# Small parts of plain weight tiles by a subtraction on VectorE, or by an accumulating transfer onto the negated large part

## Chip, cores and metric

The kernel runs on one core of a Trainium2 chip. The metric is the device time of one execution in microseconds (us), as the median of several runs.

## What is computed

A two-layer encoder trunk for 512 tokens of width 1024, all in float32. Layer 0 uses stick-breaking attention, layer 1 forgetting attention (a softmax with a running sum of log forget gates), both with 16 heads of width 64. Each layer ends with a gated feed-forward part of width 2816 that has a causal convolution of width 3. Every part is normalized before and after (RMS), and added to the residual. Cut to what matters here:

```python
a = rmsnorm(h, sb_pre_g[0])
q, k, v = split(a @ sb_w_qkv[0], 3)
h = h + rmsnorm(attention(q, k, v) @ sb_w_o[0], sb_post_g[0])
f = conv_ffn(rmsnorm(h, ffn_pre_g[0]), w_up[0], conv_w[0], conv_b[0], w_down[0])
h = h + rmsnorm(f, ffn_post_g[0])
# layer 1: q from fox_w_q (with its own norm gain), k, v and gates from w_kvf, then fox_w_o and conv_ffn
# conv_ffn(x): gate, up = split(conv(x @ w_up) + b);  (gelu(gate) * up) @ w_down
```

## The kernel before

TensorE multiplies in a fast float32 format that keeps fewer bits. To keep float32's accuracy each factor is split into two parts, a rounded large part and the small rest, and each product is made in three passes: large by large, large by small, small by large. Activations are held as AH and AL, weights as `whi` and `wlo`.

The weights come as a stream of 196 tiles of 512 KB (list `stream`, built at lines 163 to 186). A column tile holds 128 output columns for all 1024 input rows (128 partitions x 8 x 128); for the values two tiles of 4 x 256 stand in place of it. A row tile holds 128 input rows and all 1024 output columns, one run of 4 KB per partition. Row tiles serve the output projections (`sb_w_o`, `fox_w_o`) and the down-projections (`w_down`). Of the 196 tiles 172 are plain: 24 of `sb_w_qkv`, 8 of `sb_w_o`, 88 of `w_up`, 44 of `w_down`, 8 of `fox_w_o`. The 24 others (`fox_w_q`, `w_kvf`) are scaled by a norm's gain as they are split.

`make` (line 127) makes one tile: SP starts the load into `raw` (two buffers), ScalarE rounds it into `whi` (line 142), and the small part is `raw - whi`, in two halves (line 146), on VectorE, or on GpSimd for rows 1, 5 and 7 of an output projection. `whi` and `wlo` have eight buffers each (`NW`). `take` (line 157) hands a tile out and asks for the one eight further on, so tiles are made up to eight ahead, as buffers come free. A `raw` buffer is free once both parts are made.

The stages of a layer: values, queries and keys are projected (`project_v`, `project`) between the heads' steps (`head`), which alternate between TensorE, ScalarE and VectorE. Then `out_proj` runs by token blocks 0 to 3; its eight row tiles are all held to the last block. After each block, the post-norm and the next pre-norm follow, whose inverse root is computed by two small GpSimd instructions (lines 217 and 218) before VectorE and TensorE go on. The up-projection begins with three chunks over the first 256 tokens, which need blocks 0 and 1 alone. The down-projection takes one row tile per 24 matmuls.

The order of instructions on each engine is set by a scheduler that goes by a simulated timeline; on the chip each engine takes its own in that order.

Of the kernel before, what the change touches and what calls it, by code (L numbers as in the profile page):

```python
# [14 lines left out]
P = 128  # L15
# [12 lines left out]
NW = 8  # L28
EARLY = 3
POOL_ROWS = (1, 5, 7)  # L30
FILL = (4, 5)
SCALE = HD**-0.5
# Column offset of each query block's row of scores, and its width.
# [4 lines left out]
def f32(ap):  # L38
    return ap.bitcast(F32)
# [3 lines left out]
def tile_trunk(  # L43
# [29 lines left out]
    # All of PSUM, by banks. Attention: scores 0-2, weighted values 3, projections 4-5, transposes 6-7.  # L73
    # Elsewhere: pairs of banks, one for each token block or chunk of features in flight.
# [15 lines left out]
    # mask_a keeps keys before the query, mask_b those up to it.  # L90
# [10 lines left out]
    # Residual stream by token blocks; normalized activations, feature-major, in two parts.  # L101
# [9 lines left out]
    # Row p stands for head p % 16 and is of kind p % 64 // 16: kinds 0, 2 or 3, 1; less 2, 0 or 1, less 3.  # L111
# [3 lines left out]
    # ---- weight stream: each tile arrives whole and is split into two exact parts. Pool takes few of them:  # L115
    # it and DVE's operations on two operands in SBUF exclude each other. ----
# [3 lines left out]
    def col_tile(w, c0, n=P, k0=0, nk=KT, g=None):  # L120
        src = w.rearrange("(k p) c -> p k c", p=P)[:, k0 : k0 + nk, c0 : c0 + n]
        return (src, nk, n, None if g is None else g + k0, nc.vector)

    def row_tile(w, k, eng=nc.vector):
        return (w[k * P : (k + 1) * P, :].rearrange("(a p) c -> p a c", p=P), 1, D, None, eng)

    def make(i):
        src, nk, n, g, eng = stream[i]
        raw = wp.tile([P, nk, n], F32, name=f"raw{i}", tag="raw", bufs=2)
        hi = wp.tile([P, nk, n], F32R, name=f"whi{i}", tag="whi", bufs=NW)  # L130
        lo = wp.tile([P, nk, n], F32R, name=f"wlo{i}", tag="wlo", bufs=NW)
        nc.sync.dma_start(raw, src)
        if g is not None:
            for k in range(nk):
                s = gcol[:, g + k : g + k + 1]
                nc.scalar.activation(hi[:, k], raw[:, k], AF.Copy, scale=s)  # L136
                nc.vector.scalar_tensor_tensor(
                    out=lo[:, k], in0=raw[:, k], scalar=s, in1=f32(hi[:, k]), op0=ALU.mult, op1=ALU.subtract
                )
            made[i] = (hi, lo)  # L140
            return
        nc.scalar.copy(hi, raw)  # L142
        h = (nk * n) // 2
        fr, fh, fl = (t.rearrange("p k c -> p (k c)") for t in (raw, f32(hi), lo))
        for s in (slice(0, h), slice(h, 2 * h)):
            eng.tensor_tensor(out=fl[:, s], in0=fr[:, s], in1=fh[:, s], op=ALU.subtract)  # L146
        made[i] = (hi, lo)
# [22 lines left out]
    stream += [row_tile(sb_w_o[0], k, nc.gpsimd if k in POOL_ROWS else nc.vector) for k in range(KT)]  # L170
# [14 lines left out]
    stream += [row_tile(fox_w_o[0], k, nc.gpsimd if k in POOL_ROWS else nc.vector) for k in range(KT)]  # L185
    stream += ffn_stream(1)

# [27 lines left out]
    def rstd_of(ss):  # L215
        """(sum / D + eps) ** -0.5 of ss's first column, into its column 3."""
        nc.gpsimd.tensor_scalar(ss[:, 2:3], ss[:, 0:1], 1.0 / D, EPS, op0=ALU.mult, op1=ALU.add)  # L217
        nc.gpsimd.tensor_tensor(out=ss[:, 3:4], in0=ss[:, 2:3], in1=mhalf, op=ALU.pow)
        return ss[:, 3:4]

    def pre_block(b, g, t4, junk):
        """Normalizes block b of the residual and puts it into AH and AL."""
# [14 lines left out]
    def post_block(b, y, g, t4, junk):  # L237
        """Adds the normalized y to block b of the residual."""
# [8 lines left out]
    def finish(b, y, g, t4, junk):  # L247
        """post_block for the last block, by halves, with its way out."""
# [22 lines left out]
    class Attn:  # L271
# [19 lines left out]
        def gates(self):  # L291
            """Running sums of the log forget gates, and what adds fcum[t] - fcum[s] to a head's scores:
            rows (fcum in two parts, 1, 1) by query times rows (1, 1, -fcum in two parts) by key, the rows
            of all heads, 16 to a kind, in both halves of the partitions."""
# [43 lines left out]
        def gate_keys(self, p):  # L338
            """The rows by key of pair p's heads."""
            KL = self.qk[p][3]  # L340
            for o, h in ((slice(64, 128), 0), (slice(0, 64), 1)):
                s = dsel[o, 2 * p + h : 2 * p + h + 1]
                nc.gpsimd.tensor_scalar(KL[o, h, :], f32(self.MV[o]), s, 1.0, op0=ALU.mult, op1=ALU.mult)
# [56 lines left out]
        def head(self, p, hh):  # L400
# [38 lines left out]
            else:  # L439
                # exp(z), guarded where sigmoid(z) is 1 and its complement under float32's rounding.  # L440
# [79 lines left out]
    def out_proj(done, heads_end):  # L520
        """Block by block, around the last head's transposes and products."""
# [187 lines left out]
```

## Time and profile before

| what | us |
|---|---|
| median of 3 runs | 1287.02 (1283.43 to 1288.18) |
| span of the profiled execution, first to last instruction | 1282.6 |
| TensorE busy in it | 1241.5 |
| VectorE busy | 811.0 |
| ScalarE busy | 644.4 |
| GpSimd busy | 101.8 |

Of the profiled execution the span alone is recorded; it lies 4.4 us under the median. In the rows below PE is TensorE's matmuls, PEld its weight loads, DVE VectorE, ACT ScalarE, POOL GpSimd, SP the engine that starts the transfers; L146 is line 146 of the kernel. `a<-b` names the tile written and those read. Behind an arrow in square brackets stands what ended an engine's idle time, with its length ahead of it.

### The profile page before, as it was taken

Reading aid. Unit: us, or ns where it says so; the run is one execution under the profiler, and the core shown is the slowest. Engines: PE = TensorE matmul, PEld = TensorE weight load, DVE = VectorE, ACT = ScalarE, POOL = GpSimd, SP = SyncE. Lnnn points to the kernel's source line nnn. Section 1 sums busy time; section 2 is a strip of 40 time slices with the busy share of each in tenths; the row PEclk is TensorE's granted clock in tenths of the full one; section 3 lists DMA queues with packets and bytes.
Section 4 is the critical chain, followed back from the end, with each engine's and each line's share of the span. In section 5 each row is a group of like instructions: output and inputs, shape, how many; then the busy total and the mean of one; then the engine's idle time right before and its main releaser. Section 6 shows DMA issues by size and latency. Waiting matters only on the chain.

```text
span 1282.6 us, 16820 instructions
## 1 busy us (share of the span) xinstructions
PE 1241.5 (97%) x6485; PEld 1054.6 (82%) x6485; DVE 811.0 (63%) x1304; ACT 644.4 (50%) x1085; POOL 101.8 (8%) x163
## 2 busy tenths in 40 slices
PE   6999998999999999999989999999999999999998
PEld 6888886789888888888888988978988888888886
DVE  6898899576655555433478887874685555554323
ACT  5767677454433333322488786674453333333221
POOL 1000003020000000000011212342100000000001
PEclk9999999999999999999999999999999999999999
DMA  6421212124333333333223122110543233323311
GB/s 214 138 66 50 67 50 66 33 86 144 101 97 99 92 90 99 88 109 90 75 68 99 51 82 67 50 51 33 148 132 98 84 97 99 94 87 98 99 33 66
DMA packets 145928, 111.97 MB, mean 87 GB/s; under 512 B 4680, under 2 KB 136120, under 8 KB 145848
## 3 DMA queue, kind: packets, MB, share of 16 engines
q1 hardware_dynamic: 145848, 110.90, 28.8%
q8 instruction: 51, 0.84, 0.3%
q14 instruction: 29, 0.24, 0.1%
HBM read 108.79 MB, written 2.10 MB: 86 GB/s over the span
## 4 chain that ended last, share of the span: by engine, by line
PE 77%; DVE 10%; ACT 5%; DMA 4%; issue 2%; POOL 0%; SPq 0%; DVEq 0%; POOLq 0%; ACTq 0%
PE PS L211 45%; PE PS L511 21%; PE PS L389 4%; PE PS L468 2%; PE PS L409 2%; DVE wlo L146 2%; DMA raw<-sb_w_qkv_dram 2%; DVE ec L446 2%; PE PS L456 2%; DMA raw<-w_up_dram 2%; DVE ec L448 1%; DVE PL L463 1%; ACT whi L142 1%; ACT whi L136 1%; ACT ec L445 1%
## 5 line engine op out<-in xcount | busy, mean ns | idle before, releaser
L211 PE MATMUL PS<-AH,whi 128*128 128x512 f32 (+1 forms) x1088 | 402.0, 370 | 5.5 <-DVE QS L360 3.8
L211 PE MATMUL PS<-AL,whi 128*128 128x512 f32 (+1 forms) x1088 | 401.2, 369 | 0.0
L211 PE MATMUL PS<-AH,wlo 128*128 128x512 f32 (+1 forms) x1088 | 401.0, 369 | 0.0
L146 DVE TENSOR_TENSOR wlo<-raw,whi 128x512 fp32r<-128x512 f32 x332 | 217.4, 697 | 224.5 <-ACT whi L142 223.7
L142 ACT CAST whi<-raw 128x1024 fp32r<-128x1024 f32 x172 | 180.4, 1049 | 237.9 <-PE PS L211 186.4
L211 PEld LDWEIGHTS PS<-AH,whi 128*128 128x128 f32 x1088 | 204.8, 188 | 43.5 <-DVE QS L360 4.9
L211 PEld LDWEIGHTS PS<-AH,wlo 128*128 128x128 f32 x1088 | 204.5, 188 | 36.7
L211 PEld LDWEIGHTS PS<-AL,whi 128*128 128x128 f32 x1088 | 204.8, 188 | 36.2
L587 DVE SCALAR_TENSOR_TENSOR hc<-PS,cw,hc 128x511 f32<-128x511 f32 (+1 forms) x176 | 130.7, 746 | 2.7
L511 PE MATMUL PS<-whi,al 128*128 128x512 f32 x352 | 109.5, 389 | 0.0
L511 PE MATMUL PS<-whi,ah 128*128 128x512 f32 x352 | 109.3, 389 | 0.0
L511 PE MATMUL PS<-wlo,ah 128*128 128x512 f32 x352 | 109.3, 389 | 0.0
L610 DVE TENSOR_TENSOR al<-act,ah 128x512 fp32r<-128x512 f32 x44 | 30.4, 690 | 117.4 <-ACT ah L609 117.4
L609 ACT CAST ah<-act 128x512 fp32r<-128x512 f32 x44 | 27.4, 622 | 144.7 <-PE PS L511 138.5
L217 POOL TENSOR_SCALAR ss<-ss 128x1 f32<-128x1 f32 x31 | 11.7, 376 | 830.9 <-ACT junk L240 764.8
L389 PE MATMUL PS<-whi,AH 128*128 128x256 f32 x256 | 74.1, 289 | 3.5 <-DVE AL L235 1.4
L511 PEld LDWEIGHTS PS<-whi,ah 128*128 128x128 f32 x352 | 66.1, 188 | 13.7
L511 PEld LDWEIGHTS PS<-whi,al 128*128 128x128 f32 x352 | 66.1, 188 | 13.7
L511 PEld LDWEIGHTS PS<-wlo,ah 128*128 128x128 f32 x352 | 66.1, 188 | 13.7
L389 PE MATMUL PS<-wlo,AH 128*128 128x256 f32 x256 | 74.0, 289 | 0.0
L389 PE MATMUL PS<-whi,AL 128*128 128x256 f32 x256 | 73.5, 287 | 0.0
L592 ACT ACTIVATE hc<-hc 128x512 f32<-128x512 f32 x44 | 27.8, 631 | 86.3 <-DVE hc L587 86.3
(130 smaller groups left out, 1758.9 us busy)
## 6 DMA issues: line engine op xcount, KB each, us to landing
raw<-w_up_dram SPq DMA_DIRECT2D x88, 512.0 KB
raw<-w_down_dram SPq DMA_DIRECT2D x44, 512.0 KB
raw<-sb_w_qkv_dram SPq DMA_DIRECT2D x24, 512.0 KB
raw<-w_kvf_dram SPq DMA_DIRECT2D x16, 512.0 KB
raw<-sb_w_o_dram SPq DMA_DIRECT2D x8, 512.0 KB
raw<-fox_w_q_dram SPq DMA_DIRECT2D x8, 512.0 KB
raw<-fox_w_o_dram SPq DMA_DIRECT2D x8, 512.0 KB
H<-x_dram SPq DMA_DIRECT2D x4, 512.0 KB
```

Of the source, the lines that this page charges most:

```text
L142: nc.scalar.copy(hi, raw)
L146: eng.tensor_tensor(out=fl[:, s], in0=fr[:, s], in1=fh[:, s], op=ALU.subtract)
L211: nc.tensor.matmul(ps, a[:, k, :m], b[:, k, t0:t1], start=i == 0, stop=i == n - 1)
L389: nc.tensor.matmul(ps[:, o], a[:, k, sl], m[:, k % 4, :], start=i == 0, stop=i == 3 * KT - 1)
L409: nc.tensor.matmul(z[:, ZOFF[b] : ZOFF[b] + n], a[:, b * P : (b + 1) * P], m[:, :n], start=i == 0, stop=i == len(passes) - 1,)
L446: nc.vector.tensor_tensor_scan(C[:, ::-1], self.R[:, ::-1], C[:, ::-1], 0.0, ALU.mult, ALU.add)
L456: tr = nc.tensor.transpose(zt[:, o : o + P], E[:, ZOFF[b] + j * P : ZOFF[b] + (j + 1) * P], ident)
L511: mm = nc.tensor.matmul(y[:, c, :], s[:, sl], m[:, 0, c * 512 : (c + 1) * 512], start=k == 0 and i == 0, stop=k == n - 1 and i == 2,)
L587: nc.vector.scalar_tensor_tensor(out=hc[:, s:], in0=y[:, i, : T - s], scalar=col[:, 2 - s : 3 - s], in1=hc[:, s:], op0=ALU.mult, op1=ALU.add,)
L592: uses_table(nc.scalar.activation(hs[0], hs[0], AF.Gelu_apprx_tanh))
L609: nc.scalar.copy(ah, act[:, k, :])
L610: nc.vector.tensor_tensor(out=al, in0=act[:, k, :], in1=f32(ah), op=ALU.subtract)
```

## The change

The small part of a plain tile is no longer a subtraction. ScalarE writes the tile a second time, with the sign turned, as the negative large part, into `wlo`; GpSimd then starts a transfer that reads the tile from HBM once more and adds it to what stands in `wlo`. GpSimd no longer subtracts any tile; the list of rows that it took is gone. The scaled tiles are made as before. `NRAW` names the number of `raw` buffers, still two. Comments are removed, too, so lines move by one.

```diff
+NRAW = 2
 EARLY = 3
-POOL_ROWS = (1, 5, 7)
...
     def make(i):
-        src, nk, n, g, eng = stream[i]
-        raw = wp.tile([P, nk, n], F32, name=f"raw{i}", tag="raw", bufs=2)
+        src, nk, n, g = stream[i]
+        raw = wp.tile([P, nk, n], F32, name=f"raw{i}", tag="raw", bufs=NRAW)
...
         nc.scalar.copy(hi, raw)
-        h = (nk * n) // 2
-        fr, fh, fl = (t.rearrange("p k c -> p (k c)") for t in (raw, f32(hi), lo))
-        for s in (slice(0, h), slice(h, 2 * h)):
-            eng.tensor_tensor(out=fl[:, s], in0=fr[:, s], in1=fh[:, s], op=ALU.subtract)
+        nc.scalar.activation(lo, raw, AF.Copy, scale=-1.0)
+        nc.gpsimd.dma_start(lo, src, accum_op=ALU.add)
         made[i] = (hi, lo)
...
-    stream += [row_tile(sb_w_o[0], k, nc.gpsimd if k in POOL_ROWS else nc.vector) for k in range(KT)]
+    stream += [row_tile(sb_w_o[0], k) for k in range(KT)]
```

GpSimd's order at the border between the output projection and the up-projection of layer 0, before: the post- and pre-norms of blocks 1 to 3, two instructions each (`ss` is the sum of squares and its inverse root; the last pair is the pre-norm of block 3).

```order
L217 TENSOR_SCALAR ss_2484<-ss_2484 128x1
L218 TENSOR_TENSOR ss_2484<-ss_2484,mhalf_81 128x1
L217 TENSOR_SCALAR ss_2490<-ss_2490 128x1
L218 TENSOR_TENSOR ss_2490<-ss_2490,mhalf_81 128x1
L217 TENSOR_SCALAR ss_2554<-ss_2554 128x1
L218 TENSOR_TENSOR ss_2554<-ss_2554,mhalf_81 128x1
L217 TENSOR_SCALAR ss_2560<-ss_2560 128x1
L218 TENSOR_TENSOR ss_2560<-ss_2560,mhalf_81 128x1
```

The same place after the change (`wlo32` is the first tile of `w_up`):

```order
L145 DMA wlo32_2254<-w_up_dram 128x8x128
L145 DMA wlo33_2267<-w_up_dram 128x8x128
L216 TENSOR_SCALAR ss_2490<-ss_2490 128x1
L217 TENSOR_TENSOR ss_2490<-ss_2490,mhalf_81 128x1
L145 DMA wlo34_2280<-w_up_dram 128x8x128
L145 DMA wlo35_2293<-w_up_dram 128x8x128
L216 TENSOR_SCALAR ss_2554<-ss_2554 128x1
L217 TENSOR_TENSOR ss_2554<-ss_2554,mhalf_81 128x1
L145 DMA wlo36_2306<-w_up_dram 128x8x128
L145 DMA wlo37_2343<-w_up_dram 128x8x128
L216 TENSOR_SCALAR ss_2560<-ss_2560 128x1
L217 TENSOR_TENSOR ss_2560<-ss_2560,mhalf_81 128x1
```

Ahead of each of the last three norm pairs stand now two transfers.

ScalarE's order at the start of the program, before (`raw0`, `raw1` are the first two tiles, of the values' weights; `junk` is the square sum of a token block):

```order
L142 CAST whi0_100<-raw0_99 128x1024
L234 CAST AH_84<-PS_67 128x8x128
L142 CAST whi1_107<-raw1_106 128x1024
L224 ACTIVATE junk_94,ss_162<-H_83 128x1024
L234 CAST AH_84<-PS_67 128x8x128
```

And after:

```order
L143 CAST whi0_100<-raw0_99 128x1024
L144 ACTIVATE wlo0_101<-raw0_99 128x1024
L233 CAST AH_84<-PS_67 128x8x128
L143 CAST whi1_107<-raw1_106 128x1024
L144 ACTIVATE wlo1_108<-raw1_106 128x1024
L223 ACTIVATE junk_94,ss_162<-H_83 128x1024
```

The negation of each tile stands right behind its rounding, ahead of the work on the activations.

## Rows read from the trace of the kernel before

**Rows 1.** The page: span, TensorE's busy time, transfers of the hardware queue

```profile
span 1282.6 us, 16820 instructions
...
PE 1241.5 (97%) x6485; PEld 1054.6 (82%) x6485; DVE 811.0 (63%) x1304; ACT 644.4 (50%) x1085; POOL 101.8 (8%) x163
...
q1 hardware_dynamic: 145848, 110.90, 28.8%
```

**Rows 2.** Stretches: length, busy us (instructions) per engine, clock, DMA share, GB/s

```profile
0.00:52.00 52.00, 41.83 (x283) 38.28 (x284) 33.41 (x67) 28.85 (x42) 7.39 (x22) 1.00 0.61 191
52.00:262.00 210.00, 195.97 (x1120) 169.90 (x1119) 180.88 (x224) 144.80 (x199) 17.62 (x15) 0.98 0.19 57
...
300.00:530.00 230.00, 230.00 (x1053) 188.32 (x1052) 132.92 (x198) 92.82 (x115) 0.00 (x0) 1.00 0.34 99
```

**Rows 3.** One stretch of the up-projection: all engines, then line 146 alone

```profile
352.00:480.00 128.00, 128.00 (x550) 103.16 (x549) 69.65 (x104) 46.68 (x57) 0.00 (x0) 1.00 0.33 95
...
352.00:480.00 128.00, 29.66 (x46) 0.00 (x0) 1.00 0.33 95
```

**Rows 4.** Waits, of ScalarE, then of SP's queue: us in total, times, longest

```profile
ACT whi L142 <- PE PS L211: 186.4, 78, 6.4
...
ACT whi L142 <- DMA raw<-w_up_dram: 31.8, 19, 3.5
...
SPq L132 <- DVE wlo L146: 849.4, 163, 20.6
```

**Rows 5.** The page's groups: busy us, mean ns, idle before and releaser

```profile
L146 DVE TENSOR_TENSOR wlo<-raw,whi 128x512 fp32r<-128x512 f32 x332 | 217.4, 697 | 224.5 <-ACT whi L142 223.7
L142 ACT CAST whi<-raw 128x1024 fp32r<-128x1024 f32 x172 | 180.4, 1049 | 237.9 <-PE PS L211 186.4
```

**Rows 6.** Line 132, SP's issue of the w_up loads: ns least, median, most

```profile
L132 SPq DMA_DIRECT2D raw<-w_up_dram x88: 367/368/379, 208.7 to 1103.0; - x88
```

**Rows 7.** Groups of GpSimd's instructions by shape, whole span

```profile
L146 POOL TENSOR_TENSOR wlo<-raw,whi 128x512 fp32r<-128x512 f32 x12 | 16.1, 1356 | 163.3 <-DVE QS L360 121.3 <-ACT whi L142 35.1 <-PE PS L456 6.9
```

**Rows 8.** Start, in order of time: start us, length us, engine, line, operation

```profile
9.41 1.04 ACT L142 CAST whi<-raw 128x1024 fp32r<-128x1024 f32 x1 [0.29 <-DMA raw<-sb_w_qkv_dram]
...
11.27 1.29 DVE L146 TENSOR_TENSOR wlo<-raw,whi 128x512 fp32r<-128x512 f32 x2
...
14.12 0.41 PE L389 MATMUL PS<-wlo,AH 128*128 128x256 f32 x1
...
27.09 1.05 ACT L142 CAST whi<-raw 128x1024 fp32r<-128x1024 f32 x1 [2.22 <-DMA raw<-sb_w_qkv_dram]
30.10 1.05 ACT L142 CAST whi<-raw 128x1024 fp32r<-128x1024 f32 x1 [1.96 <-DMA raw<-sb_w_qkv_dram]
```

**Rows 9.** Border to the up-projection of layer 0, by engine, in order of time

```profile
267.88 2.01 ACT L142 CAST whi<-raw 128x1024 fp32r<-128x1024 f32 x2
...
277.19 1.06 ACT L142 CAST whi<-raw 128x1024 fp32r<-128x1024 f32 x1 [3.48 <-DMA raw<-w_up_dram]
...
286.42 1.05 ACT L142 CAST whi<-raw 128x1024 fp32r<-128x1024 f32 x1 [1.76 <-DMA raw<-w_up_dram]
...
271.49 2.49 DVE L146 TENSOR_TENSOR wlo<-raw,whi 128x512 fp32r<-128x512 f32 x4
...
288.60 0.24 POOL L217 TENSOR_SCALAR ss<-ss 128x1 f32<-128x1 f32 x1 [5.79 <-ACT junk L224]
...
278.42 0.36 PE L211 MATMUL PS<-AH,whi 128*128 128x256 f32 x1
...
290.85 1.09 PE L232 MATMUL PS<-ident,t 128*128 128x128 f32 x8 [1.82 <-DVE t L229]
```

**Rows 10.** VectorE's group of line 146 in stick-breaking attention, 52 to 262 us

```profile
L146 DVE TENSOR_TENSOR wlo<-raw,whi 128x512 fp32r<-128x512 f32 x34 | 24.5, 763 | 2.6 <-ACT whi L142 2.5
```

More of the change, by code (lines that the diff above doesn't have):

```diff
@@ L121, in col_tile, with row_tile @@
         src = w.rearrange("(k p) c -> p k c", p=P)[:, k0 : k0 + nk, c0 : c0 + n]
-        return (src, nk, n, None if g is None else g + k0, nc.vector)
-    def row_tile(w, k, eng=nc.vector):
-        return (w[k * P : (k + 1) * P, :].rearrange("(a p) c -> p a c", p=P), 1, D, None, eng)
+        return (src, nk, n, None if g is None else g + k0)
+    def row_tile(w, k):
+        return (w[k * P : (k + 1) * P, :].rearrange("(a p) c -> p a c", p=P), 1, D, None)
     def make(i):
-        src, nk, n, g, eng = stream[i]
-        raw = wp.tile([P, nk, n], F32, name=f"raw{i}", tag="raw", bufs=2)
+        src, nk, n, g = stream[i]
+        raw = wp.tile([P, nk, n], F32, name=f"raw{i}", tag="raw", bufs=NRAW)
         hi = wp.tile([P, nk, n], F32R, name=f"whi{i}", tag="whi", bufs=NW)
@@ L184, in tile_trunk @@
             stream += qk if pr else qk + v if g else v + qk
-    stream += [row_tile(fox_w_o[0], k, nc.gpsimd if k in POOL_ROWS else nc.vector) for k in range(KT)]
+    stream += [row_tile(fox_w_o[0], k) for k in range(KT)]
     stream += ffn_stream(1)
```

## Prediction

> **What bounds the kernel now.** I read the page first, then stretches cut at the stage borders, then the waits, then two stretches in order of time. TensorE is busy for 1241.5 us of a span of 1282.6 us [rows 1]: 41.1 us are idle, and no change on another engine can win more than these and what is stretched inside the busy time. The stages differ. In the up-projection of layer 0 (300 to 530 us) TensorE is busy in all 230.00 us, VectorE in 132.92 and ScalarE in 92.82 [rows 2]: TensorE sets the end alone, and a lighter VectorE buys nothing there. The same holds for the down-projections. In the first 52 us TensorE lacks 10.2 us and the DMA engines are 0.61 busy; in stick-breaking attention (52 to 262 us) it lacks 14.0 us of 210 and VectorE is at 180.88 us, 86% [rows 2]. Only there is VectorE a suspect. Forgetting attention (640 to 880 us) takes scaled tiles, which the change leaves alone but for the eight row tiles of the output projection.
>
> How far the weights run ahead comes from the waits. ScalarE waited 186.4 us for TensorE before it rounded a large part, and 31.8 us for the transfers of w_up [rows 4]. It mostly waits for a free buffer, not for data, so the eight buffers are full and a tile has several tile periods between being made and being used. In 352 to 480 us 46 half-tile subtractions ran, 23 tiles in 128 us: one tile in 5.57 us [rows 3]. With eight in hand a small part may come 30 us later than now and nobody in that stage notices. What counts there is the rate, not the delay.
>
> **What goes.** Of the 172 plain tiles 166 lose two VectorE subtractions: 332 of 697 ns, 217.4 us of VectorE [rows 5]. The other six lose two GpSimd ones, 12 of 1356 ns, 16.1 us [rows 7]. On the path that sets the end this is worth something only in stick-breaking attention: 34 subtractions, 24.5 us of VectorE [rows 10].
>
> **What comes on ScalarE.** A negated copy per tile, priced as the rounding copy beside it, 1.05 us [rows 5]: 172 x 1.05 = 180 us. In the up-projection ScalarE goes from 92.8 us to about 92.8 + 44 x 1.05 = 139 of 230: hidden under TensorE. In stick-breaking attention 19 or 20 tiles add some 20 us to 144.80 of 210 [rows 2]: ScalarE becomes the fuller one (165) while VectorE falls to 156. A buffer of raw weights comes free after two ScalarE copies (2.1 us) instead of a copy, a hand-over and two subtractions (1.05 + 1.4 and a wait; SP waited 849.4 us for the subtractions [rows 4]), so loads may start a little sooner.
>
> **What comes on the DMA engines.** The tile's bytes cross from HBM a second time: 172 x 0.524 MB = 90 MB on top of 110.90 [rows 1]. A load costs 0.33 x 128 / 23 = 1.84 us of all 16 engines [rows 3]. Below, the accumulating transfer costs the same; above, twice that, 3.67 us, since it reads two places (weights and old content) for each one it writes. Load and accumulation make 3.7 to 5.5 us per tile against a period of 5.57: 66 to 99% of the engines. I take the upper value, and it just fits; any further cost per piece does not.
>
> The Trainium skill ("Collectives: The Full Stack", Part 3, the fold count) says that a DMA reduction halves the rate because the add needs two source reads, 32.35 against 62.28 GB/s. No run here shows it yet; by that rule the accumulation is 3.67 us, the top of my bounds, and it speaks against this change.
>
> **What comes on GpSimd.** It issues 172 transfers, 112 of them in many short pieces (column tiles 1024 of 512 bytes). No row shows what that holds it. SP issues a transfer of this shape in 0.37 us [rows 6], the lower bound. The nearest GpSimd work is a pass over half a tile, 1.36 us [rows 7]; two make 2.7 us, which I take, since software must walk every piece. It decides at 5.57 us, the tile period; that is the upper bound for the forecast, and beyond it lies a rival.
>
> The Trainium skill ("DMA: Bandwidth & Descriptors", Anatomy of one DMA) calls descriptor generation small and variable, with many descriptors before the incremental cost shows. By that rule GpSimd is never the bound and the forecast's sum is some 2 us per issue kinder.
>
> **Where the delay is not hidden: the start.** Now the first large part is begun at 9.41, the first small parts end near 12.6, and TensorE takes one at 14.12 [rows 8]. After: 10.45 + 1.05 (negation) + 0.37 to 2.7 (issue) + about 4.4 (a transfer: the load that follows the release near 272.8 is in use at 277.19 [rows 9]) = 16.3 to 18.6, so 2 to 4.5 us late. Then the engines: 0.61 x 52 = 31.7 us busy now [rows 2]; the 13 tiles of that stretch add 24 to 48 us, against 20.3 idle. That costs 4 to 28 us if all were needed at once; but about eight are only prefetched, and rounding copies already come just every 3 us or so [rows 8]. I take +8, bounds 0 and +28.
>
> **The two borders before the up-projections.** All eight row tiles of the output projection are held to its last block, so the first w_up tiles are made late: large parts at 267.88 and then 277.19, first used at 278.42 [rows 9]. The small part would be there at about 270 + 0.4 to 2.7 + 4.4 = 275 to 277 if no other transfer is in the way: just in time. GpSimd is the other place. The order shows two transfers ahead of each of the last three pairs of norm instructions. The last norm step now begins at 288.60 on GpSimd, and TensorE stood idle 1.82 us for it before 290.85 [rows 9], so each us there goes to the end. The sixth tile's negation would end near 288.5; its issue then holds the norm by 0.4 to 2.7 us, the fifth tile's likewise, and late loads add to it; loads that start sooner give some back. +5 per border, bounds 0 and +12: +10 for two.
>
> **Stick-breaking attention.** VectorE gives back 24.5 us, ScalarE takes about 20 on the same chain of head steps. Idle TensorE time caps the gain at 14.0 us [rows 2]; I take -6, bounds -14 and +10 (ScalarE's copies in front of a head's step).
>
> **Sum.** 8 + 10 - 6 = +12 on 1282.6, a span of about 1295. The median of the runs is 4.4 us above that span; 1299 us. Up- and down-projections, forgetting attention and the tail: 0, covered by the tiles in hand.
>
> **The rivals.**
> A. *The tile rate breaks* (slower, by far). Either an accumulated tile costs the DMA engines more than 3.7 us (short pieces, the reading back of the old content) or its issue holds GpSimd over 5.57 us. Then the projections run at that rate. Against: the sums above just fit. For: they fit by 0.1 us. GpSimd at 6.5 us costs 88 x 0.9 = +80 us (w_up tiles alone); an accumulation at three loads makes 4 x 1.84 = 7.4 per tile, 132 x 1.8 = +238; GpSimd at 10 us, +390. Middle about +170, 1455 us.
> B. *The relief decides* (faster). VectorE's chain in stick-breaking attention shortens by the whole 14 us, the start costs 4 and the borders nothing as loads start sooner: 1277 us. For: VectorE 86% busy there; against: ScalarE follows on the same chain.
> C. *Nothing visible.* Rates hold, start and borders cost about what attention gains, or the second transfer is as cheap as a plain load: 1281 to 1293 us.
>
> **Chances.** About 0.5% is what a measurement of this kernel can tell from no change: 1280.6 to 1293.5. The forecast case, rates hold and the unhidden delays outweigh the relief (1285 to 1320): 0.45, of which 0.10 within the 0.5%. Rival A 0.35, B 0.12, C 0.08. Slower 0.70, same 0.18, faster 0.12. The forecast's own range is 1285 to 1320. The range for 8 in 10 must reach into A: up to 1510 leaves about 0.10 above, and 1277 about 0.10 below.
>
> **What the new profile would show.** Rates hold: TensorE fully busy from 300 to 530 us, the DMA share there under 1 (0.66 to 0.99 by my bounds), ScalarE still waiting for TensorE before it rounds. Rival A: TensorE idle between column tiles, waiting for the transfer into the small part, with DMA share at its top or GpSimd's queue full. The start: TensorE's first use of a small part 2 to 5 us later. The borders: the last norm instruction on GpSimd behind a transfer, TensorE idle for more than 1.82 us. Attention: a stage of less than 210 us, VectorE near 156. I am wrong if TensorE idles in the projections, or if the start costs nothing.

## The result and the profile after the change

The changed kernel takes **1324.87 us** (median of four runs, 1323.51 to 1326.94); beside it the kernel before took 1285.90 us (four runs, 1283.43 to 1288.18). The ratio is 1.031 [1.029, 1.033]: slower by 39 us, where 12 were forecast. The sign held; the time lies above the forecast's own range (1285 to 1320), though inside the range for 8 in 10 (1277 to 1510), which had to reach into rival A. The profiled executions differ by 41.9 us, and on these the account below is made.

The page of the kernel after: span, busy time of the engines, transfers by queue (GpSimd's is `software_dynamic`; packets, MB, time of the packets as a share of 16 engines' span), then the groups of large parts, negations and issues (busy us, mean ns, idle before):

```profile
span 1324.5 us, 16853 instructions
...
PE 1259.6 (95%) x6485; PEld 1068.4 (81%) x6485; DVE 608.0 (46%) x972; ACT 804.9 (61%) x1257; POOL 310.2 (23%) x323
...
q0 software_dynamic: 121024, 90.19, 48.9%
q1 hardware_dynamic: 145848, 110.90, 28.1%
...
L143 ACT CAST whi<-raw 128x1024 fp32r<-128x1024 f32 x172 | 180.1, 1047 | 190.0 <-PE PS L210 110.4
...
L144 ACT ACTIVATE wlo<-raw 128x1024 fp32r<-128x1024 f32 x172 | 181.4, 1055 | 84.7 <-PE PS L510 72.2
...
L145 POOL DMA_DIRECT2D wlo<-w_up_dram x88 | 136.9, 1555 | 311.3 <-ACT wlo L144 309.2
...
L145 POOL DMA_DIRECT2D wlo<-w_down_dram x44 | 37.9, 861 | 198.9 <-ACT wlo L144 194.0
```

Three readings, against [rows 1, 5]. VectorE fell by 203 us, ScalarE rose by 160.5, GpSimd by 208.4: the work moved as the change says. TensorE runs the same 6485 matmuls, but is busy 18.1 us longer, and idle for 64.9 us in place of 41.1. So of 41.9 us more, 23.8 are idle time and **18.1 are the same matmuls taking longer**. A sum made of idle time alone misses nearly half. The clock granted to TensorE tells where most of the 18.1 come from: its mean over the whole execution fell from 0.996 to 0.983, and 1.3% of 1324.5 us are 17 us.

Where it was lost is read from the first or last instruction of each stage, in us from the span's start:

| mark | before | after | later by | of it in this stage |
|---|---|---|---|---|
| first exponential, layer 0 | 52.1 | 71.0 | 18.9 | 18.9 |
| last exponential, layer 0 | 226.9 | 245.0 | 18.1 | -0.8 |
| last matmul of the output projection | 277.4 | 295.5 | 18.1 | 0 |
| first matmul of the down-projection | 528.1 | 554.0 | 25.9 | 7.8 |
| last matmul of the down-projection | 648.5 | 674.3 | 25.8 | 0 |
| first exponential, layer 1 | 700.3 | 727.5 | 27.2 | 1.4 |
| last exponential, layer 1 | 867.5 | 899.3 | 31.8 | 4.6 |
| last matmul of the output projection | 907.7 | 940.4 | 32.7 | 0.9 |
| first matmul of the down-projection | 1156.6 | 1198.4 | 41.8 | 9.1 |
| last matmul of the down-projection | 1276.1 | 1317.8 | 41.7 | 0 |
| end | 1282.6 | 1324.5 | 41.9 | 0.2 |

The exponentials' line, before and after (least, median, most ns; start of the first and the last):

```profile
L442 ACT ACTIVATE ec<-PS x16: 1219/1242/1266, 52.1 to 226.9; 128x1280 f32<-128x1280 f32 x16
```

```profile
L441 ACT ACTIVATE ec<-PS x16: 1216/1225/1263, 71.0 to 245.0; 128x1280 f32<-128x1280 f32 x16
```

**The start** loses 18.9 us. Stretches of the kernel after (columns as in [rows 2]):

```profile
0.00:52.00 52.00, 30.95 (x203) 28.85 (x204) 12.46 (x24) 27.89 (x35) 19.32 (x29) 0.97 1.12 238
...
0.00:71.00 71.00, 46.80 (x285) 41.89 (x285) 18.91 (x42) 40.53 (x55) 25.21 (x34) 0.98 1.13 232
71.00:245.00 174.00, 165.56 (x959) 145.05 (x960) 139.26 (x166) 146.08 (x194) 33.99 (x24) 0.96 0.62 122
...
295.00:325.00 30.00, 23.42 (x166) 22.41 (x166) 6.24 (x5) 13.75 (x16) 10.81 (x10) 0.89 1.29 230
...
352.00:480.00 128.00, 128.00 (x550) 103.13 (x549) 47.02 (x65) 75.28 (x90) 38.70 (x25) 1.00 1.18 204
```

In 71 us TensorE does what it did in 52 [rows 2] (285 matmuls against 283) and is busy 46.80 us of them: 14 us more idle, 5 more busy. The DMA share of the first 52 us is 1.12, from 0.61. The transfers that TensorE waited for up to 72 us (us in total, times, longest):

```profile
PE PS L649 <- DMA crow<-conv_w_dram: 4.6, 1, 4.6
PE PS L388 <- DMA wlo<-sb_w_qkv_dram: 3.9, 1, 3.9
PE PS L649 <- DMA raw<-sb_w_qkv_dram: 1.4, 1, 1.4
...
PE PS L210 <- DMA wlo<-sb_w_qkv_dram: 1.0, 1, 1.0
```

Beside them stand 9.4 us for the norm of the first blocks, as in the kernel before, and 1.3 us and less for others of VectorE's results. Of these four waits only two are for a small part. The largest is for `crow`, the convolution's rows, which the change does not touch. ScalarE's large parts in the same stretch, in order of time, show the loads late as well:

```profile
30.68 1.05 ACT L143 CAST whi<-raw 128x1024 fp32r<-128x1024 f32 x1 [1.70 <-DMA raw<-sb_w_qkv_dram]
...
36.22 1.05 ACT L143 CAST whi<-raw 128x1024 fp32r<-128x1024 f32 x1 [2.63 <-DMA raw<-sb_w_qkv_dram]
...
43.06 1.04 ACT L143 CAST whi<-raw 128x1024 fp32r<-128x1024 f32 x1 [4.83 <-DMA raw<-sb_w_qkv_dram]
```

They stand 5.5 and 6.8 us apart, against 3.0 before [rows 8].

**The borders** lose 7.8 and 9.1 us. The first, by engine, in order of time:

```profile
299.65 1.05 ACT L143 CAST whi<-raw 128x1024 fp32r<-128x1024 f32 x1 [5.06 <-DMA raw<-w_up_dram]
...
302.20 1.56 POOL L145 DMA_DIRECT2D wlo<-w_up_dram  x1 [5.71 <-ACT wlo L144]
303.83 0.19 POOL L216 TENSOR_SCALAR ss<-ss 128x1 f32<-128x1 f32 x1
...
301.80 0.39 PE L210 MATMUL PS<-AH,wlo 128*128 128x256 f32 x1 [1.86 <-DMA wlo<-w_up_dram]
...
311.88 0.38 PE L210 MATMUL PS<-AH,wlo 128*128 128x256 f32 x1 [2.86 <-DMA wlo<-w_up_dram]
```

The six accumulating transfers that GpSimd begins from 287.5 to 310.3 us need longer from issue to landing than those of the whole program (7.8 us in the middle case, below):

```profile
DMA to landing us min/median/max: 8.3/10.4/12.4
```

With 0.90 and 0.96 us later on, TensorE waits 6.6 us here for small parts, 7.4 at the second border. The matmuls of the up-projection, grouped, for the kernel before (277 to 528 us) and after (295 to 554 us):

```profile
L211 PE MATMUL PS<-AH,wlo 128*128 128x512 f32 (+1 forms) x400 | 147.2, 368 | 0.0
```

```profile
L210 PE MATMUL PS<-AH,wlo 128*128 128x512 f32 (+1 forms) x400 | 148.7, 372 | 6.6 <-DMA wlo<-w_up_dram 6.6
```

The three passes together take 445.0 us of modelled, overlapping time in place of 441.8: 3.2 more. In 295 to 325 us the granted clock is 0.89, a mean of the two levels of 1.2 and 2.4 GHz, and TensorE is busy for 23.42 us. The first 30 us of that stage before, for comparison:

```profile
277.00:307.00 30.00, 28.18 (x238) 27.81 (x237) 18.17 (x25) 14.16 (x17) 1.61 (x4) 1.00 0.51 151
```

There the clock is full. Waits of 6.6, slower matmuls of about 3.2, less the 1.82 us for the norm [rows 9], which is gone: 8.0, against 7.8 measured. The second border goes the same way: 7.4 + 1.9 - 0.8 = 8.5, against 9.1.

**The steady stages** lose nothing: in 352 to 480 us TensorE is busy in all 128.00 us, as in [rows 3].

### The profile page after: what moved, and what is told of

The parts are those of the page before. It is cut to its first block, busy times and chain, and to the rows that moved or that the text cites. A ratio compares the mean times of both kernels' runs of the same rounds, so it can differ in the third digit from the quotient of the medians.

```text
span 1324.5 us, 16853 instructions
## 1 busy us (share of the span) xinstructions
PE 1259.6 (95%) x6485; PEld 1068.4 (81%) x6485; DVE 608.0 (46%) x972; ACT 804.9 (61%) x1257; POOL 310.2 (23%) x323
## 3 DMA queue, kind: packets, MB, share of 16 engines
q0 software_dynamic: 121024, 90.19, 48.9%
q1 hardware_dynamic: 145848, 110.90, 28.1%
## 4 chain that ended last, share of the span: by engine, by line
PE 68%; DMA 4%; ACT 4%; DVE 1%; issue 1%; POOL 0%; DVEq 0%; POOLq 0%; ACTq 0%
PE PS L210 41%; PE PS L510 20%; PE PS L388 3%; DMA raw<-w_up_dram 2%; DMA wlo<-w_up_dram 2%; PE PS L467 1%; PE PS L408 1%; PE PS L455 1%; ACT whi L135 1%; ACT whi L143 1%; ACT wlo L144 1%; ACT ec L428 0%; DVE wlo L136 0%; DMA raw<-fox_w_q_dram 0%; ACT t L226 0%
## 5 line engine op out<-in xcount | busy, mean ns | idle before, releaser
L210 PE MATMUL PS<-AH,wlo 128*128 128x512 f32 (+1 forms) x1088 | 405.3, 373 | 15.0 <-DMA wlo<-w_up_dram 14.0
L210 PE MATMUL PS<-AH,whi 128*128 128x512 f32 (+1 forms) x1088 | 406.1, 374 | 4.6 <-DVE QS L359 2.8
L143 ACT CAST whi<-raw 128x1024 fp32r<-128x1024 f32 x172 | 180.1, 1047 | 190.0 <-PE PS L210 110.4
L210 PEld LDWEIGHTS PS<-AH,wlo 128*128 128x128 f32 x1088 | 208.2, 191 | 54.2 <-DMA wlo<-w_up_dram 15.9
L210 PEld LDWEIGHTS PS<-AH,whi 128*128 128x128 f32 x1088 | 208.2, 192 | 42.8 <-DVE QS L359 3.5
L210 PEld LDWEIGHTS PS<-AL,whi 128*128 128x128 f32 x1088 | 208.6, 192 | 36.4
L144 ACT ACTIVATE wlo<-raw 128x1024 fp32r<-128x1024 f32 x172 | 181.4, 1055 | 84.7 <-PE PS L510 72.2
L145 POOL DMA_DIRECT2D wlo<-w_up_dram x88 | 136.9, 1555 | 311.3 <-ACT wlo L144 309.2
L145 POOL DMA_DIRECT2D wlo<-w_down_dram x44 | 37.9, 861 | 198.9 <-ACT wlo L144 194.0
L510 PEld LDWEIGHTS PS<-wlo,ah 128*128 128x128 f32 x352 | 66.1, 188 | 13.8
L462 DVE TENSOR_TENSOR PL<-PS,PH 128x512 fp32r<-128x512 f32 (+1 forms) x96 | 56.4, 596 | 26.5 <-ACT PH L461 25.5
```

The lines of the kernel that those rows point to most:

```text
L144: nc.scalar.activation(lo, raw, AF.Copy, scale=-1.0)
L145: nc.gpsimd.dma_start(lo, src, accum_op=ALU.add)
L210: nc.tensor.matmul(ps, a[:, k, :m], b[:, k, t0:t1], start=i == 0, stop=i == n - 1)
L462: nc.vector.tensor_tensor(out=PL[:, :o], in0=zt[:, :o], in1=f32(PH[:, :o]), op=ALU.subtract)
L510: mm = nc.tensor.matmul(y[:, c, :], s[:, sl], m[:, 0, c * 512 : (c + 1) * 512], start=k == 0 and i == 0, stop=k == n - 1 and i == 2,)
```

## The experiments

All but e9 are made on the kernel before, whose `make` gets a second branch for some tiles; the tiles are numbered as in the stream: 0 to 3 are taken first, 0 to 12 are made before attention starts, 13 to 31 within stick-breaking attention and its output projection, 32 to 39 at the first border, 122 to 129 are the rows of `fox_w_o`, 130 to 137 stand at the second border. The branch:

```diff
         nc.scalar.copy(hi, raw)
+        if COND:
+            nc.scalar.activation(lo, raw, AF.Copy, scale=-1.0)
+            nc.gpsimd.dma_start(lo, src, accum_op=ALU.add)
+            made[i] = (hi, lo)
+            return
```

COND is given for each; the scheduler orders each kernel anew, which alone shifts a stage by one to three us: the length of stick-breaking attention (first to last exponential) was 173.7, 175.7 and 177.3 us in the three kernels below that change nothing in tiles 13 to 31, against 174.8 before. A difference of that size in one stage is not read by itself. Forgetting attention varies likewise: 168.5 and 168.6 us in these three kernels, against 167.2 before.

### Which places cost: e1, e2, e3

**e1.** Only the start goes back to the subtraction.

```diff
+        if i > 12:
```

> The first 13 tiles of the stream (those made in the first 52 us) are made by subtraction again, all other plain tiles by the accumulating transfer. Theory: 18.9 us of the loss arise before the first exponential of the scores (71.0 us after, 52.1 before), because the second transfers of these tiles crowd the loads and the first small parts come late; then the first exponential is back at 52 to 55 us and the time is about 1307 us (18 less than the changed kernel). Rival: the loss belongs to the steady stream of second transfers, and the start only shows a share of it; then tiles 13 and on still crowd, the first exponential stays above 60 us and less than 8 us come back.

1312.31 us, ratio 1.0213 [1.0193, 1.0232]. The exponentials of e1:

```profile
L447 ACT ACTIVATE ec<-PS x16: 1213/1244/1260, 51.2 to 234.1; 128x1280 f32<-128x1280 f32 x16
```

The first comes at 51.2 us, so the whole 18.9 come from tiles 0 to 12. But the end gains 10.4 us of the span only: stick-breaking attention now takes 182.9 us, 8 more than before. That loss lay hidden in the changed kernel, where the stage is 174.0 us long. Of the 8.9 us between the two, 3.8 are TensorE work that had been done ahead of the late first exponential (169.35 us busy and 985 matmuls in the stage here, 165.56 us and 959 there); the other 5 I can't place. The time is 5 us above the 1307 that I expected, for this reason.

**e2.** Only the eight tiles at each border go back.

```diff
+        if not (32 <= i < 40 or 130 <= i < 138):
```

> Of w_up, the first eight tiles of each layer are made by subtraction again, all other plain tiles by the accumulating transfer. Theory: the two borders cost 7.8 and 9.1 us since these tiles' small parts come 8 us after their issue and GpSimd's norm steps stand behind their issues; both come back, about 1308 us (17 less). Rival: the borders are late because loads of raw tiles are slow beside any second transfer, and because ScalarE has one more copy per tile; then at most half comes back, 1316 us or more.

1308.56 us, ratio 1.0189 [1.0167, 1.0211]. From the last matmul of the output projection to the first of the down-projection the loss is 2.6 and 0.8 us, in place of 7.8 and 9.1. The waits for `wlo` are gone, and the norm is waited for again, 2.94 us at the first border. So the accumulation of these sixteen tiles was the cause. The run takes away their late small parts, what their transfers cost the loads beside them, ScalarE's copies and GpSimd's issues ahead of the norms all at once, and does not share the loss out among these.

**e3.** Start, borders and the rows of `fox_w_o` go back; 135 of 172 tiles still accumulate (the 130 of the expectation is a miscount).

```diff
+        if i > 12 and not (32 <= i < 40 or 130 <= i < 138) and not 122 <= i < 130:
```

> Subtraction for the first 13 tiles, for the first eight w_up tiles of each layer and for the fox_w_o tiles; the accumulating transfer for the rest (130 of 172 plain tiles, among them all of steady up- and down-projection). Theory: the rate of the stream holds and only those three places cost; 1286 us, within 5 of the kernel before. Rival: the rate itself costs (accumulation 3.77 us and load 1.8 us of the DMA engines per tile against a period of 5.57): 1295 us or more.

1290.69 us, ratio 1.0049 [1.0032, 1.0066]: between the theory's 1286 and the rival's 1295. The exponentials of both layers in e3, then TensorE at its first border:

```profile
L447 ACT ACTIVATE ec<-PS x16: 1220/1242/1257, 50.6 to 233.1; 128x1280 f32<-128x1280 f32 x16
...
L434 ACT ACTIVATE ec<-PS,st x64: 349/529/705, 705.3 to 872.9; 128x512 f32<-128x512 f32 x16, 128x256 f32<-128x256 f32 x16, 128x384 f32<-128x384 f32 x16, 128x128 f32<-128x128 f32 x16
...
297.38 1.97 PE L237 MATMUL PS<-ident,t 128*128 128x128 f32 x8 [3.19 <-DVE t L234]
```

Forgetting attention is back at 167.6 us (before 167.2, after 171.8), so its loss hung on the eight row tiles. The projections with their 116 accumulated tiles keep their rate. What remains is stick-breaking attention, 182.5 us.

### Why stick-breaking attention loses: e4, e6, e5, e10

**e4.** Only tiles 13 to 31 are accumulated.

```diff
+        if 13 <= i < 32:
```

> The accumulating transfer only for tiles 13 to 31 (stick-breaking attention after the start, and its output projection); subtraction everywhere else. Theory: VectorE is lighter by some 20 us in this stage and ScalarE heavier by as much, on the same chain of head steps, so nothing is won: 1286 us, within 4. Rival: VectorE's relief shortens the stage by 6 us or more: 1280 or less.

1289.39 us, ratio 1.0047 [1.0028, 1.0066]. The exponentials, and two stretches in which TensorE first waits and then works:

```profile
L447 ACT ACTIVATE ec<-PS x16: 1221/1242/1257, 50.8 to 233.6; 128x1280 f32<-128x1280 f32 x16
...
192.00:200.00 8.00, 2.37 (x16) 1.86 (x15) 6.00 (x5) 7.95 (x12) 1.72 (x2) 0.83 0.56 123
200.00:208.00 8.00, 7.93 (x33) 6.66 (x34) 5.93 (x9) 2.92 (x5) 0.00 (x0) 0.75 0.53 142
```

The loss is there with these tiles alone: 182.8 us. Part of the 8 us is work that moved into the stage (981 matmuls, 966 before); the last matmul of the output projection is 5.3 us later than before, at 282.7 us. For e1 and e3 it is 6.2 and 5.2 us. From 192 to 200 us ScalarE is busy in 7.95 of 8 us while TensorE has 2.37; in the next 8 us TensorE is full, but its clock is granted at 0.75 on average. Here ScalarE holds the chain.

**e6.** The negated copy alone: ScalarE writes it into `lo`, and the subtraction then overwrites it. No second transfer.

```diff
+        if 13 <= i < 32 or 122 <= i < 130:
+            nc.scalar.activation(lo, raw, AF.Copy, scale=-1.0)
         h = (nk * n) // 2
```

> Small parts by subtraction everywhere, as in the kernel before, but for tiles 13 to 31 and fox_w_o ScalarE first writes the negated copy into the small part's buffer, which the subtraction then overwrites: the copy's cost without a second transfer. Theory: 27 copies of 1.05 us, on the chain of head steps; stick-breaking attention grows from 175 to 182 us or more (VectorE keeps its subtractions, so rather more than less), forgetting attention by some 3 us; 1290 or more. Rival: copies are hidden and the transfers cost; 1284 to 1287.

1302.09 us, ratio 1.0143 [1.0112, 1.0173].

```profile
L444 ACT ACTIVATE ec<-PS x16: 1223/1240/1268, 53.0 to 241.6; 128x1280 f32<-128x1280 f32 x16
```

188.6 us, 13.8 more than before, from nineteen copies (20.1 us in all) and the subtractions that come later behind them, with no accumulation and no relief of VectorE. In forgetting attention the copies alone cost 4.1 us.

**e5.** The accumulation, with the negation on GpSimd in place of ScalarE.

```diff
+        if 13 <= i < 32 or 122 <= i < 130:
+            nc.gpsimd.tensor_scalar(lo, f32(hi), -1.0, 1.0, op0=ALU.mult, op1=ALU.mult)
+            nc.gpsimd.dma_start(lo, src, accum_op=ALU.add)
+            made[i] = (hi, lo)
+            return
```

> The accumulating transfer for tiles 13 to 31 and for the fox_w_o tiles, the negative large part written by GpSimd from the large part and not by ScalarE from the raw tile; subtraction everywhere else. Theory: the 7 to 8 us that stick-breaking attention lost with the transfers in tiles 13 to 31 alone, and the 4 us of forgetting attention, are ScalarE's extra copies on the chain of head steps; without them the stages are back at 175 and 167 us or below, time 1283 or less. Rival: the second transfers themselves (late small parts, GpSimd's issues) cost; then stick-breaking attention stays at 181 us or more and the time at 1289 or more.

1280.17 us, ratio 0.9966 [0.9946, 0.9986].

```profile
L447 ACT ACTIVATE ec<-PS x16: 1221/1242/1251, 50.6 to 222.0; 128x1280 f32<-128x1280 f32 x16
```

171.4 us. So with the same transfers, moving 20 us of copies off ScalarE is worth 11.4 us against e4, and the stage ends below that of the kernel before. (GpSimd reads the large part, so a `raw` buffer also comes free one copy earlier; that share is not separated.) Forgetting attention still takes 171.8 us, 4.6 more than before, though ScalarE has no copies there.

**e10.** As e5, for tiles 13 to 31 alone; the rows of `fox_w_o` keep the subtraction.

```diff
+        if 13 <= i < 32:
+            nc.gpsimd.tensor_scalar(lo, f32(hi), -1.0, 1.0, op0=ALU.mult, op1=ALU.mult)
+            nc.gpsimd.dma_start(lo, src, accum_op=ALU.add)
```

> The accumulating transfer for tiles 13 to 31 alone (stick-breaking attention after the start, and its output projection), with GpSimd writing the negative large part; subtraction elsewhere, fox_w_o too. Theory: stick-breaking attention keeps the 3.4 us that it won with this negation (171.4 against 174.8 us from the first to the last exponential), and forgetting attention loses nothing: 1278 to 1281, below both kernels. Rival: what was won comes back later (order of the borders), or the forgetting stage was not the transfers' doing: 1283 or more.

1279.14 us, ratio 0.9953 [0.9936, 0.9970]: **faster than both kernels**, by half a per cent. Its exponentials, and GpSimd's negations (ns least, median, most):

```profile
L447 ACT ACTIVATE ec<-PS x16: 1221/1241/1257, 50.4 to 220.6; 128x1280 f32<-128x1280 f32 x16
...
L144 POOL TENSOR_SCALAR wlo<-whi x19: 1034/1626/3014, 53.7 to 210.8; 128x1024 fp32r<-128x1024 f32 x19
```

170.2 us, 4.6 less than before; forgetting attention takes 168.7. With e5 this is the second kernel below all that leave the stage alone (173.7 us at least), so the relief of VectorE shows where ScalarE does not pay for it. Not all of the gain is that: the profiled span is 6.7 us shorter, and 3.0 of it come between the down-projection of layer 0 and layer 1's first exponential, a place that the edit does not touch and where e4 and e5 gain 1.8 and 2.9.

### What the start pays for: e7, e8, e12, e9

**e7.** Only the first four tiles are accumulated.

```diff
+        if i < 4:
```

> The accumulating transfer for the first four tiles alone. Of the 18.9 us at the start, the delay of the first small parts (first use 4 us late) and not the crowding by later tiles is meant to be seen here. Theory: delay gives 4 to 6 us, the first exponential at 56 to 58 us, time about 1288; the rest is crowding. Rival: nearly all comes from the first tiles (the order of the matmuls waits at each of them): first exponential at 66 us or later, 1297 or more.

1298.74 us, ratio 1.0116 [1.0084, 1.0148]. Exponentials, then TensorE's two longest waits for transfers:

```profile
L447 ACT ACTIVATE ec<-PS x16: 1219/1241/1267, 68.0 to 243.7; 128x1280 f32<-128x1280 f32 x16
...
19.23 0.58 PE L394 MATMUL PS<-wlo,AH 128*128 128x256 f32 x1 [5.06 <-DMA wlo<-sb_w_qkv_dram]
...
45.15 0.38 PE L655 MATMUL PS<-ident,crow 88*128 88x88 f32 x1 [4.92 <-DMA crow<-conv_w_dram]
```

The first exponential comes at 68.0: four tiles make 15.9 us of the 18.9. I had thought that they cost 4 to 6, and was wrong.

**e8.** Only the next nine.

```diff
+        if 4 <= i < 13:
```

> The accumulating transfer for tiles 4 to 12 alone. Theory: their second transfers take the DMA engines 9 x 3.77 = 34 us in a stretch where the loads alone have 0.61 of them, so loads come late and the first exponential stands at 62 us or later, 10 to 14 us behind; time 1293 to 1298. Rival: they are only prefetched and cost nothing at the start; first exponential at 52 to 55 us, time within 4 of the kernel before.

1300.68 us, ratio 1.0137 [1.0101, 1.0172]. Exponentials, TensorE's longest wait beside the norm's (`V` are the values), and ScalarE in order of time:

```profile
L447 ACT ACTIVATE ec<-PS x16: 1220/1242/1265, 62.7 to 240.0; 128x1280 f32<-128x1280 f32 x16
...
PE PS L216 <- DVE V L400: 6.3, 1, 6.3
...
37.32 1.06 ACT L142 CAST whi<-raw 128x1024 fp32r<-128x1024 f32 x1 [5.71 <-DMA raw<-sb_w_qkv_dram]
...
41.05 1.04 ACT L142 CAST whi<-raw 128x1024 fp32r<-128x1024 f32 x1 [1.72 <-DMA raw<-sb_w_qkv_dram]
...
42.96 0.58 ACT L399 CAST V<-PS 128x128 fp32r<-128x128 f32 x3
```

10.6 us, so these are not free either, though they are prefetched. TensorE waits for no small part here. The loads come late beside the second transfers, ScalarE stands still for one of them, and the values' casts, which follow in ScalarE's order, come at 42.96 us in place of 34.27 before; VectorE and TensorE wait for these. 15.9 + 10.6 is more than 18.9: the two overlap.

**e12.** Crowding without waiting: the first four tiles are subtracted as before, and the same copies and accumulating transfers go into a spare tile that nobody reads.

```diff
         for s in (slice(0, h), slice(h, 2 * h)):
             eng.tensor_tensor(out=fl[:, s], in0=fr[:, s], in1=fh[:, s], op=ALU.subtract)
+        if i < 4:
+            scr = pre[0].tile([P, nk, n], F32R, name=f"scr{i}", bufs=1)
+            nc.scalar.activation(scr, raw, AF.Copy, scale=-1.0)
+            nc.gpsimd.dma_start(scr, src, accum_op=ALU.add)
```

> The first four tiles get their small parts by subtraction, as in the kernel before; beside that ScalarE also writes a negated copy of each into a spare tile, and GpSimd starts the accumulating transfer onto it, which nobody reads. So the four transfers, their issues and the copies are all there, but no matmul waits for them. With the small parts of these four tiles by the transfer the first exponential stood at 68.0 us and the span was 1299.3. Theory: the start is late because the transfers crowd the loads of the next tiles; then the first exponential is at 60 us or later here too and the time 1292 or more. Rival: it is late because the matmuls wait for the small parts (and what stands behind them in order); then the first exponential is at 52 to 56 us and the time within 4 of the kernel before.

1293.86 us, ratio 1.0062 [1.0041, 1.0082]. Exponentials, and TensorE's longest wait for a transfer:

```profile
L447 ACT ACTIVATE ec<-PS x16: 1217/1240/1265, 58.5 to 232.2; 128x1280 f32<-128x1280 f32 x16
...
36.59 0.38 PE L656 MATMUL PS<-ident,crow 88*128 88x88 f32 x1 [3.69 <-DMA crow<-conv_w_dram]
```

6.4 us. Of the 15.9 of e7 about 6.4 are crowding (the transfers, with the four copies), and the other 9.5 go, by this difference, to TensorE's waits for the small parts and what is late behind them. The wait for `crow` belongs to the crowding: it is here without any `wlo` being late.

**e9.** The changed kernel with four buffers for the convolution's rows in place of two, so that their loads may start sooner.

```diff
-                t = pool.tile([2 * nb, P], F32, name="crow")
+                t = pool.tile([2 * nb, P], F32, name="crow", bufs=4)
```

> The changed kernel with four buffers in place of two for the rows of the convolution weights, so that their small loads are issued ahead of the raw tiles at the start. Theory: of the 18.9 us lost at the start some 5 are TensorE standing idle for such a load, which waits on SP's queue behind raw loads that the second transfers hold up; the first exponential moves from 71 to 64 to 66 us and the time to about 1319. Rival: that wait covers another (the weights would have been late anyway): first exponential at 69 us or later, time within 2 us of the changed kernel.

1338.73 us, ratio 1.0419 [1.0394, 1.0444]. Exponentials, and TensorE's longest wait for a transfer:

```profile
L441 ACT ACTIVATE ec<-PS x16: 1219/1242/1267, 72.1 to 257.7; 128x1280 f32<-128x1280 f32 x16
...
34.02 0.58 PE L210 MATMUL PS<-AH,wlo 128*128 128x256 f32 x1 [7.03 <-DMA wlo<-sb_w_qkv_dram]
```

The 4.6 us wait for `crow` is gone and nothing came of it: a wait of 7.03 us for a small part stands in its place, and the first exponential comes later, at 72.1. That fits transfers that are the limit together, so that an earlier one makes another late; it is not shown by itself. Stick-breaking attention takes 185.6 us here, 11 more than in the changed kernel; this kernel was not followed further.

### All tiles with GpSimd's negation: e11

The changed kernel's plan for all 172 tiles (no condition), negated on GpSimd as in e5.

> The changed kernel with the negative large part written by GpSimd instead of ScalarE, for all plain tiles. Theory: start and borders stay late (about 19 and 17 us or rather more, since GpSimd's negation takes longer than ScalarE's and stands before the norms), stick-breaking attention wins 3 us: 1318 to 1330. Rival: ScalarE's copies were the cause of the late start and borders too: 1300 or less.

1325.37 us, ratio 1.0321 [1.0296, 1.0346], as the changed kernel.

```profile
L447 ACT ACTIVATE ec<-PS x16: 1217/1240/1252, 72.3 to 244.5; 128x1280 f32<-128x1280 f32 x16
```

The start is as late as with ScalarE's negation (72.3), and the borders lose 9.3 and 11.3 us, so taking the copies off ScalarE does not bring these places back; stick-breaking attention takes 172.2 us.

## Why the prediction was right or wrong, step by step

**Tiles in hand and rate: right, the rate in part by luck.** The forecast stood on tiles in hand and on a rate that just fits. The tiles were in hand and the rate was kept: TensorE is full through the projections after the border, and ScalarE still waits 110.4 us for TensorE before it rounds, so the buffers are mostly full there. Rival A, a broken rate (0.35), did not come. But the sum behind it did not hold: from 352 to 480 us the DMA share is 1.18 with 25 accumulations begun, so load and accumulation make about 1.18 x 128 / 25 = 6.0 us per tile, 4.2 of it the accumulation (the load was 1.84). That is above the top of the bounds (3.67) and above the period of 5.57, where the forecast said that any further cost would not fit. It did fit, because such a sum of packet times is no limit (last section).

**Prices: right to within a few per cent, but for two.** The negated copy was 1.05 us, and is 1.055. The accumulating transfer was put at 3.67 us of all 16 engines, the upper bound; as a mean of all tiles, 48.9% of 1324.5 us over 172 tiles is 3.77, against 1.76 for half a MB of plain load (28.1% of 1324.5 us over 110.90 MB, times 0.524). The Trainium skill ("Collectives: The Full Stack", Part 3, the fold count) says that a DMA add needs two source reads and so runs at half the rate; the trace agrees on the rate, with 2.1 times; no run shows the reads. GpSimd's issue is 1.55 us for a column tile and 0.86 for a row tile, where I took 2.7. The time from issue to landing was put at 4.4 us from a load; for the accumulating transfer it is, over line 145 of the kernel after:

```profile
DMA to landing us min/median/max: 5.2/7.8/13.8
```

7.8 us, so a small part comes 3.4 us later than I allowed for, in the middle case.

**The start: the term that was mis-sized most.** Forecast +8, measured +18.9, within its bounds of 0 and 28. Two steps failed. A first small part 2 to 4.5 us late was the direct cost I reckoned; e7 shows 15.9 us for four tiles, of which e12 leaves 9.5 to the lateness and 6.4 to the crowding. And "about eight are only prefetched" took nine tiles nearly off the bill; e8 shows 10.6 for these alone, by late loads that hold ScalarE and so the values behind them, a path that the forecast had not looked at. The DMA engines' sum itself was about right: the packets' time in the first 52 us rose from 31.7 us to 1.12 x 52 = 58, by 26, forecast 24 to 48 against 20.3 idle. I weighed that as a chance of delay only. Which transfer TensorE then waits for is a matter of order (e9).

**The borders: right place, wrong mechanism.** Forecast +5 each, bounds 0 and 12; measured 7.8 and 9.1. "Just in time" failed: with 8.3 to 12.4 us to landing, in place of 4.4, and loads that come later themselves (5.06 us of waiting by ScalarE at 299.65), TensorE waited four and five times for small parts. The norm behind GpSimd's issues, which I thought the other place, cost nothing: the norm's instruction at 303.83 does stand right behind an issue of 1.56 us, but TensorE waits for weights then, and for the norm at neither border. Whether late landing alone or late loads alone would have been enough no run separates. And no term stood for the clock: 30 us with TensorE's waits had a mean clock of 0.89, worth about 3 us at the first border.

**Stick-breaking attention: wrong sign, hidden by the late start.** Forecast -6 (bounds -14 and +10), measured -0.8 in the changed kernel; but with the start in time it is +8 (e1, e3, e4). The failing step is "ScalarE takes about 20 on the same chain", which I set off against VectorE's 24.5 by busy totals. On this chain the copies, with the subtractions later behind them, cost 13.8 us for 20 (e6). The relief is there, some 3 to 6 us: 182.8 with copies and accumulation against 188.6 with copies and subtraction; 170.2 and 171.4 with the negation elsewhere against 174.8. VectorE fell about as forecast (by 24.5), from 160.90 us between 52 and 227 us before to 139.26 between 71 and 245. The rival B, relief deciding, needs the copies elsewhere: that is e10.

**Forgetting attention: forecast 0, measured +4.6,** with 1.4 and 0.9 more around it. The eight row tiles that I mentioned and then left at nothing are the cause (e3), though some 1.4 of the 4.6 may be the new order alone, as in e7, e8 and e12. How the loss is shared out stays open: the copies alone make 4.1 (e6), and with GpSimd's negation and no copies it is still 4.6 (e5), so two different burdens on that stretch cost about the same. The stretch itself, before and after (columns as in [rows 2]), tells only in what form the time went:

```profile
700.00:868.00 168.00, 165.03 (x998) 145.35 (x997) 135.93 (x301) 126.90 (x330) 47.33 (x66) 1.00 0.20 60
```

```profile
727.00:900.00 173.00, 168.27 (x997) 147.56 (x996) 128.06 (x290) 134.45 (x337) 45.78 (x68) 0.97 0.34 83
```

Of 5.0 us more, 1.8 are idle and 3.2 are as many matmuls taking longer, at a granted clock of 0.97 in place of 1.00.

**Sum.** The forecast was 8 + 10 - 6 = 12. Measured: 18.9 + 16.9 - 0.8 + 6.9 = 41.9, with the 6.9 being what lies around and in forgetting attention. Of the 30 missing, 11 are the start, 7 the borders, 5 the relief that did not come, 7 forgetting attention. Each term but the last stayed within its bounds; all of them erred towards too little, and their upper bounds together (28 + 24 + 10) were not given a chance of their own: the forecast's case ended at 1320, and the next slower case, rival A, had its middle at 1455. The 4.4 us from span to median also joined one quick execution to a median; in the changed kernel the profiled execution's time is 1.7 us above its span.

**What stays open.** Where 5 of the 8.9 us go by which attention is shorter behind a late start, the split in forgetting attention, the split at the borders between late landing and late loads, and the split of e12's crowding between the four copies and the transfers.

## What to carry to other kernels

A longer delay costs nothing where tiles run ahead, and shows where they don't: before replacing a short engine step by a transfer, list the places where the buffers are empty (the start, each border behind a stage that holds its tiles) and keep the old way there; with subtraction at the start, the borders and in one output projection, 32 of 39 us were gone. Look also at what stands behind a waiting copy in its engine's order: a late load that nobody needs yet can hold work that is needed now (e8). Work taken off one engine of a chain should go to an engine that is not on that chain: the same accumulation gained 0.5% with GpSimd's negation in attention and lost 0.5% with ScalarE's. And here the stalls were dearer than their idle time, since matmuls around them ran at a lower granted clock (0.89 at the first border, 0.75 in e4); count the stretched busy time too.

## What the runs showed of the chip

- The DMA share of a stretch went over 1: 1.18 in 352 to 480 us and 1.29 in 295 to 325, with two queues in use. The packets of the loads took no longer for it (28.8% of 1282.6 us before, 28.1% of 1324.5 us after: 369 and 372 us), so the times of the two queues' packets overlap. The share is then no measure of what is left, and my sign for a kept rate, "under 1", was a wrong reading: TensorE was full at 1.18.
- GpSimd's issue of an accumulating transfer holds it for 1.55 us with 1024 pieces of 512 bytes and for 0.86 us with 128 runs of 4 KB, against SP's 0.37 us for a load [rows 6].
- TensorE's clock fell behind short idleness: 2.37 us of work in 8, then 8 us of nearly full work at 0.75 (e4). Behind the single wait of 1.82 us at the border of the kernel before it stayed at 1.00 (277 to 307 us).
